# First half of the mixer's output projection: three bf16 terms and six products in place of two float32r terms and three

## The chip, the cores and the metric

One core of a Trainium2 chip runs the whole program. Its engines work side by side, each from a queue of its own: TensorE (in the profile PE for the products and PEld for loading the stationary operand), VectorE (DVE), ScalarE (ACT), GpSimd (POOL) and SyncE (SP), which here only starts transfers. The time is that of the device in microseconds (us) from the start to the end of one execution; lower is better. A comparison of two kernels uses several executions of each on the same chip.

## The reference

One inference step of a decoder layer (one layer) for a prompt of 512 tokens and 8 samples of 8 tokens, so 576 tokens in all, with 1024 features. The part that matters here is the mixer's output projection:

```python
u = _rms(x) * g_pre_mix
proj = u @ w_in
...
y_ssd = _rms(y_ssd.reshape(bsz, length, SSM_GROUPS, SSM_INNER // SSM_GROUPS)).reshape(bsz, length, SSM_INNER) * g_ssm_out
...
h_ml = _rms(h_ml).reshape(bsz, length, ML_INNER) * g_mlstm_out * jax.nn.sigmoid(og)
mix = jnp.concatenate([y_ssd.astype(x.dtype), h_ml.astype(x.dtype)], axis=-1) @ w_out
x = x + _rms(mix) * g_post_mix
```

`w_out` has 2048 rows and 1024 columns. Its first 1024 rows meet the output of the state-space heads (`y_ssd`), the last 1024 that of the mLSTM heads (`h_ml`). Everything is in float32, and the outputs are compared with a float32 computation. After the mixer come a cross attention and a gated feed-forward network (SwiGLU), both with projections of the same kind.

## The kernel before, in words

All activations lie feature by feature: 128 features on the partitions, 8 tiles of them, and the 576 tokens along the free axis. A large product is done in float32r with each operand as two terms: `hi` is the operand copied to a float32r tile on ScalarE, `lo` is the operand minus `hi`, made on VectorE (`split`, line 191, for activations, `split_w`, line 173, for weights). `gemm` (line 195) then issues three products for each input tile of 128 features: weight hi by activation hi (line 201), weight hi by activation lo (line 202), weight lo by activation hi (line 203). Each of them loads its stationary weights anew. The tokens go in two parts, 256 and 320 wide (`HALVES`), because a bank of PSUM holds 512 columns; `gemm2` (line 206) runs `gemm` for a part and evacuates the bank.

`split_w` takes a buffer `raw` (two of them) for the loaded float32 weights, and a pair `whi`, `wlo` (three pairs) of 128x1024. The load is issued on the SP queue. With `cut=1024` the whole subtraction is VectorE's.

The first half of the output projection is the loop at line 1133. For each of 8 output tiles it loads the weights' first 1024 rows (`I["wout"][j, 0]`, 8 input tiles of 128x128), splits them, runs both token parts, one in a bank of the pool `pg` (`GP`) and one in a bank of `pa` (`MP`), three banks in each, and copies each bank to `f_mix` on ScalarE (line 1136, `evs`). Its operand is `mixs`, the state-space output after its norm: `gn_apply` (line 1014) multiplies `y` by gain and norm row (line 1017) and splits it into `mixs_h` and `mixs_l` (line 1018). `mixs_h` lies in a pool on the right side (`big0`, line 1007) that opens where the pool of the mLSTM samples closes (its last operation is line 1002), `mixs_l` in slot 2 of the big buffers.

In the same loop `presplit` splits weights of later stages and writes the low terms to DRAM; it goes by the evacuations (`evs`). From the fifth output tile on, transfers of the memory inputs (`memraw`, line 1143) are issued behind the weight loads. The second half (`out2`, line 1166) adds the mLSTM rows: it multiplies `mixm_h` and `mixm_l` by the other 1024 rows of the weights, adds the bank to `f_mix` (line 1161) and collects sums of squares for the norm behind it (`ssqo`, line 1162, and `ssqm` for the memory, line 1150). It stays as it is.

Around this loop the order of the instructions on each engine is made by a planner that simulates the program and takes what is ready, in the order of the source; products into different banks are thus interleaved. Further on, from the second half of the attention's output projection, the order on each engine is written out by hand.

Of the kernel before, what the change touches and what calls it, by code (L numbers as in the profile page):

```python
# [11 lines left out]
F32 = mybir.dt.float32  # L12
F32R = mybir.dt.float32r
BF16 = mybir.dt.bfloat16
AF = mybir.ActivationFunctionType
ALU = mybir.AluOpType
# [3 lines left out]
P = 128  # L20
T = 576
# [3 lines left out]
KT = 8  # L25
# [3 lines left out]
HALVES = [(0, 256), (256, 320)]  # L29
# [87 lines left out]
def build(nc, tc, ctx, I, O):  # L117
    V, A, G, S, TE = nc.vector, nc.scalar, nc.gpsimd, nc.sync, nc.tensor
    mm = TE.matmul

    cp = ctx.enter_context(tc.tile_pool(name="const", bufs=1))
    wp = ctx.enter_context(tc.tile_pool(name="weights", bufs=1))
# [8 lines left out]
    def SL(slot, name, dt=F32, shape=(P, KT, T)):  # L131

        return big.tile(list(shape), dt, name=name, tag="s%d" % slot, bufs=1)
# [37 lines left out]
    loads = []  # L171

    def split_w(src, n=1024, cut=CUT, acc=False, pool=None, to=None, raw=None):
        if raw is None:
            raw = wp.tile([P, 1024], F32, name="raw", tag="raw", bufs=2)
        loads.append(S.dma_start(raw[:, :n], src))
        if to:
            split(*to, raw[:, :n])
            return to
        hi, lo = [(pool or wp).tile([P, 1024], F32R, name=k, tag=k, bufs=NWX if pool else 3) for k in ("whi", "wlo")]  # L180
        A.copy(hi[:, :n], raw[:, :n])  # L181
        for e, a, b in ((V, 0, cut), (G, cut, n)):
            if b > a and e is G and acc:

                A.activation(lo[:, a:b], hi[:, a:b].bitcast(F32), AF.Copy, scale=-1.0)  # L185
                G.dma_start(lo[:, a:b], src[:, a:b], accum_op=ALU.add)  # L186
            elif b > a:
                e.tensor_tensor(lo[:, a:b], raw[:, a:b], hi[:, a:b].bitcast(F32), op=ALU.subtract)  # L188
        return hi, lo

    def split(hi, lo, src, eng=None):
        A.copy(hi, src)
        (eng or V).tensor_tensor(lo, src, hi.bitcast(F32), op=ALU.subtract)
# [12 lines left out]
    def gemm2(units, xh, xl, evac, name, halves=(0, 1), alloc=None, order=None, parts=HALVES):  # L206
        for i in halves:
            t0, n = parts[i]
            ps = (alloc or GP)(name)[:, :n]
            m = gemm(ps, units, xh, xl, t0, n, order=order)  # L210
            evac(t0, n, ps)
        return m

    def act(t):
        return lambda k, t0, n: t[:, k, t0:t0 + n]


    pows, ssq_mm, rops, rows = [], [], [], []
# [124 lines left out]
    stop = gemm(ps0[2][1], [(*w2, KT)], U, UL, 256, 320, 0, NSS)  # L343
# [12 lines left out]
    stop = gemm(ps0[3][0], [(*w3, KT)], U, UL, 0, 256)  # L356
# [208 lines left out]
    y = xs  # L565
# [98 lines left out]
    for g in range(2):  # L664
        ps = BP("ps_xts")
# [5 lines left out]
    ps = BP("ps_bts")  # L671
# [7 lines left out]
    for g in range(2):  # L679
        for hb in range(2):  # L680
            dst = cpad[:, g, 4 * hb:4 * hb + 4, :].rearrange("p b t -> p (b t)")
            src = bc[:, 2 + g, TP + 32 * hb:TP + 32 * hb + 32]
# [4 lines left out]
    for g in range(2):  # L687
        psb = BP("ps_ls")
        pb3 = psb.rearrange("p (h t) -> p h t", h=8)
        for h in range(8):  # L690
            mm(psb[:, h * TS:(h + 1) * TS], sel[:80, 8 * g + h:8 * g + h + 1].to_broadcast([80, P]), cumst[:, TP:T],
               start=h == 0, stop=h == 7, skip_group_check=True)
# [8 lines left out]
        for h in range(8):  # L701
            k, j = h % 2, (8 * g + h) // 2
# [6 lines left out]
    ps = BP("ps_eg")  # L709
# [6 lines left out]
    for b in range(4):  # L716
# [3 lines left out]
        for g in range(2):  # L720
            for hb in (1, 0):
# [3 lines left out]
                   start=b == 0, stop=b == 3, skip_group_check=True)  # L725
        for hb in range(2):
# [4 lines left out]
            for g in range(2):  # L731
                ps = BP("ps_hu")
# [6 lines left out]
    ps = BP("ps_yt")  # L739
# [88 lines left out]
    for h in range(4):  # L828
        q, k = qk[:, h, :], qk[:, 4 + h, :]
# [16 lines left out]
        for c in range(4):  # L846
# [3 lines left out]
                        op=ALU.mult)  # L850
# [16 lines left out]
        f = head_norm(num, expnm[:, :, h:h + 1].rearrange("p c o -> p (c o)"), 4, mp_, "p")  # L867
# [89 lines left out]
    for hb in range(2):  # L957
# [6 lines left out]
        for b in range(4):  # L964
# [16 lines left out]
            for h in range(4):  # L981
                ps = BP("ps_cu")
# [13 lines left out]
        f = head_norm(num, ex, 1, ms, "s")  # L996
# [9 lines left out]

    big0 = ctx.enter_context(tc.tile_pool(name="big0", bufs=1, side="right", reuse_waits="tile"))

    def SL0(name, dt=F32R):
        return big0.tile([P, KT, T], dt, name=name, tag="s0", bufs=1)  # L1010

    mixs_h = SL0("mixs_h")
    mixs_l = SL(2, "mixs_l", F32R)
    def gn_apply(g):
        rb = gn_rc[g][0][:, 0:T]
        for j in range(4 * g, 4 * g + 4):
            V.scalar_tensor_tensor(y[:, j, :], y[:, j, :], PAR("g_ssm", j), rb, op0=ALU.mult, op1=ALU.mult)
            split(mixs_h[:, j, :], mixs_l[:, j, :], y[:, j, :])


    mixm_h = SL(3, "mixm_h", F32R)
# [77 lines left out]
    f = SL(5, "f_mix")  # L1099
# [8 lines left out]
    evs, ahead = [], []  # L1108
# [22 lines left out]
    rmem_b = at.tile([P, 256], F32, name="rmem_b")  # L1131
    ssqm, ssq = ssq_tile("ssqm"), ssq_tile("ssqo")
    for j in range(8):
        w = split_w(I["wout"][j, 0], cut=1024)
        for i, bank in enumerate((GP, MP)):
            gemm2([(*w, KT)], act(mixs_h), act(mixs_l), lambda t0, n, ps: evs.append(A.copy(f[:, j, t0:t0 + n], ps)),
                  "ps_o1", (i,), bank)
        presplit(1 if j else 2)

        if j > 3:  # L1140
            k2 = slice(2 * j - 8, 2 * j - 6)
            with tc.issue_after(loads[-1].ins):
                S.dma_start(memraw[:, k2, :], I["memT"][:, k2, :])
# [26 lines left out]
    x = SL(1, "x1")  # L1170
# [39 lines left out]
    m = out2(7, 0)  # L1210
    with tc.issue_after(m.ins):
        rc = rstd_cols([ssq], HCHUNKS[1], "po1", alloc=B0)
    m = out2(6, 0)
# [170 lines left out]
    mk, m = mem_key(3, wm[:2])  # L1384
    with tc.issue_after(m.ins):
        rc = rstd_cols([ssq], HCHUNKS[0], "po0", alloc=B0)
    mv, m = mem_value(3, wm[2:])
# [10 lines left out]
    m = xq(4, 1)  # L1398
    with tc.issue_after(m.ins):
        rc2[1] = rstd_cols([ssq2], HCHUNKS[1], "p21", alloc=B1)  # L1400
    m = xq(5, 1)
    with tc.issue_after(m.ins):
        rstd_rows(rc2[1][:, 2:3], CHUNKS[4:], rb2, B1)
    m = xq(6, 1)
# [34 lines left out]
    f = SL(4, "f_xo")  # L1439
# [250 lines left out]
    class Pair:  # L1690
# [72 lines left out]
        def bank(s):  # L1763
            return (MP if s.up else GP)("ps_u" if s.up else "ps_g")[:, :288]
# [726 lines left out]
```

## Time and profile before

| what | value |
|---|---|
| median of 3 runs | 1104.03 us (1101.62 to 1104.86) |
| the profiled execution: its own time | 1104.28 us |
| its span, first to last instruction | 1102.5 us |
| products (MATMUL) and loads (LDWEIGHTS) | 8351 each |
| busy: PE, PEld | 1089.3 us, 1042.0 us |
| busy: DVE, ACT, POOL | 771.4, 604.0, 215.3 us |
| first half of the projection (396.82 to 447.87 us) | 51.05 us, 384 products |
| second half (447.70 to 502.40 us) | 54.70 us |

In a row of the profile stand the line of the source, the engine, the operation, the tiles as output<-input, the shape as output<-input, and xN for the number of instructions. A row of the timeline begins with the start and the duration in us, counted from the span's start. A group's row ends with the busy time, the mean duration in ns, and the idle time in front of it with what ended it. A row of one tile has the least, median and greatest duration in ns and the first and last start in us. The duration of a product is the time until its result is there; products overlap, so the cost of one is the distance to the next start.

### The profile page before, as it was taken

The page shows a single profiled execution, that of the slowest core. Times are in us where ns is not written, and L with a number is a line of the kernel's source. Part 1 is how long each engine was busy: PE and PEld are TensorE (multiplying, and loading weights), DVE is VectorE, ACT ScalarE, POOL GpSimd, SP SyncE. Part 2 cuts the span into 40 slices and gives each one's busy share as a digit, 9 for nine tenths or more (in the row PEclk, how much of TensorE's full clock was granted, in tenths as well). Part 3 has the DMA queues.
Part 4 walks back from the last instruction along what each step waited for, and adds up shares of the span by engine and source line. Part 5 has one row for each costly group of instructions (what it writes and reads, how often), then busy time and mean ns, then how long its engine had stood idle before and what let it go on. Part 6 is the DMA issues. An engine that isn't in the chain of part 4 may idle for free.

```text
span 1102.5 us, 21225 instructions
## 1 busy us (share of the span) xinstructions
PE 1089.3 (99%) x8351; PEld 1042.0 (95%) x8351; DVE 771.4 (70%) x1521; ACT 604.0 (55%) x1121; POOL 215.3 (20%) x301
## 2 busy tenths in 40 slices
PE   9999999999999999999999999999999999999997
PEld 8999889898998999999988889999999999999997
DVE  6797765558786784578755556676578879888655
ACT  6768523246563465566535445634565556555654
POOL 1333442323122121110144401100000210020000
PEclk9999999999999999999999999999999999999999
DMA  6776553425474438773477755652552863497432
GB/s 205 178 148 154 121 160 126 155 83 158 130 202 108 127 99 287 284 278 100 154 272 268 287 168 169 208 184 66 179 152 82 203 161 89 102 230 211 108 133 86
DMA packets 59432, 182.34 MB, mean 165 GB/s; under 512 B 6556, under 2 KB 10780, under 8 KB 58820
## 3 DMA queue, kind: packets, MB, share of 16 engines
q1 hardware_dynamic: 44324, 142.19, 38.4%
q0 software_dynamic: 14720, 38.28, 16.6%
q8 instruction: 65, 1.06, 0.4%
q10 hardware_dynamic: 288, 0.52, 0.1%
q14 instruction: 35, 0.29, 0.1%
HBM read 151.66 MB, written 29.30 MB: 164 GB/s over the span
## 4 chain that ended last, share of the span: by engine, by line
PE 82%; DVE 5%; DMA 4%; ACT 3%; issue 1%; POOL 0%; DVEq 0%; ACTq 0%; SPq 0%
PE ps_in L201 5%; PE ps_in L202 5%; PE ps_in L203 5%; PE ps_g L1770 3%; PE ps_g L1771 3%; PE ps_g L1772 3%; PE ps_u L1770 3%; PE ps_u L1771 3%; PE ps_u L1772 3%; PE ps_o L201 2%; PE ps_o L203 2%; PE ps_o L202 2%; PE ps_dn L201 2%; PE ps_dn L203 2%; PE ps_dn L202 2%; PE ps_dn L1978 2%
## 5 line engine op out<-in xcount | busy, mean ns | idle before, releaser
L203 PE MATMUL ps_in<-uh,wlo 128*128 128x256 f32 (+1 forms) x544 | 163.8, 301 | 0.7 <-DMA wlo<-win 0.4
L202 PE MATMUL ps_in<-ul,whi 128*128 128x256 f32 (+1 forms) x544 | 163.9, 301 | 0.0
L201 PE MATMUL ps_in<-uh,whi 128*128 128x256 f32 (+1 forms) x544 | 163.7, 301 | 0.0
L181 ACT CAST whi<-raw 128x1024 fp32r<-128x1024 f32 (+1 forms) x102 | 102.7, 1011 | 83.5 <-PE ps_in L202 28.7
L188 DVE TENSOR_TENSOR wlo<-raw,whi 128x512 fp32r<-128x512 f32 (+1 forms) x94 | 91.2, 972 | 50.6 <-ACT whi L181 48.8
L202 PEld LDWEIGHTS ps_in<-ul,whi 128*128 128x128 f32 x544 | 103.0, 189 | 2.9 <-issue 2.2
L203 PEld LDWEIGHTS ps_in<-uh,wlo 128*128 128x128 f32 x544 | 103.0, 190 | 2.4 <-DVE wlo L188 0.6
L201 PEld LDWEIGHTS ps_in<-uh,whi 128*128 128x128 f32 x544 | 103.0, 189 | 2.0 <-issue 0.8
L186 POOL DMA_DIRECT2D wlo<-win x32 | 28.0, 883 | 80.8 <-ACT wlo L185 64.2
L1770 PE MATMUL ps_g<-b,whi 128*128 128x288 f32 x144 | 42.5, 296 | 0.2 <-ACT cc L1829 0.2
L1771 PE MATMUL ps_u<-b,whi 128*128 128x288 f32 x144 | 42.5, 295 | 0.0
L1771 PE MATMUL ps_g<-b,whi 128*128 128x288 f32 x144 | 42.5, 295 | 0.0
L1770 PE MATMUL ps_u<-b,whi 128*128 128x288 f32 x144 | 42.5, 295 | 0.0
L201 PE MATMUL ps_xo<-qh,whi 128*128 128x288 f32 x128 | 38.3, 302 | 0.4 <-ACT whi L181 0.3
L203 PE MATMUL ps_o<-mixm_h,wlo 128*128 128x256 f32 (+1 forms) x128 | 38.1, 298 | 0.0
L201 PE MATMUL ps_o<-mixm_h,whi 128*128 128x256 f32 (+1 forms) x128 | 38.0, 297 | 0.0
L202 PE MATMUL ps_o<-mixm_l,whi 128*128 128x256 f32 (+1 forms) x128 | 37.9, 296 | 0.0
L203 PE MATMUL ps_xq<-u2h,wlo 128*128 128x320 f32 (+1 forms) x128 | 37.9, 296 | 0.0
L202 PE MATMUL ps_xq<-u2l,whi 128*128 128x320 f32 (+1 forms) x128 | 37.8, 297 | 0.0
L201 PE MATMUL ps_xq<-u2h,whi 128*128 128x320 f32 (+1 forms) x128 | 37.8, 300 | 0.0
L202 PE MATMUL ps_xo<-ql,whi 128*128 128x288 f32 x128 | 37.7, 295 | 0.0
L203 PE MATMUL ps_xo<-qh,wlo 128*128 128x288 f32 x128 | 37.5, 295 | 0.0
(785 smaller groups left out, 3895.3 us busy)
## 6 DMA issues: line engine op xcount, KB each, us to landing
raw<-win SPq DMA_DIRECT2D x35, 512.0 KB, 3.6
raw<-wout SPq DMA_DIRECT2D x17, 512.0 KB, 5.6
raw<-wxq SPq DMA_DIRECT2D x13, 512.0 KB, 3.7
raw<-wgate SPq DMA_DIRECT2D x13, 512.0 KB, 4.4
raw<-wup SPq DMA_DIRECT2D x13, 512.0 KB, 4.0
wlo<-win POOLq DMA_DIRECT2D x24, 256.0 KB, 5.6
kva<-kc SPq DMA_DIRECT2D x12, 512.0 KB, 6.5
kva<-vc SPq DMA_DIRECT2D x12, 512.0 KB, 6.6
```

What stands on the lines that cost most here:

```text
L181: A.copy(hi[:, :n], raw[:, :n])
L186: G.dma_start(lo[:, a:b], src[:, a:b], accum_op=ALU.add)
L188: e.tensor_tensor(lo[:, a:b], raw[:, a:b], hi[:, a:b].bitcast(F32), op=ALU.subtract)
L201: mm(ps, wh, ah, start=i == 0, stop=False)
L202: mm(ps, wh, al, start=False, stop=False)
L203: m = mm(ps, wl, ah, start=False, stop=i == len(tiles) - 1)
L1770: mm(ps, wh, b[0][:, k, :], start=start and k == 0, stop=False, skip_group_check=True)
L1771: mm(ps, wh, b[1][:, k, :], start=False, stop=False, skip_group_check=True)
L1772: m = mm(ps, wl, b[0][:, k, :], start=False, stop=k == 3, skip_group_check=True)
L1978: mm(ps, wh, bh, start=start and k == 0, stop=False, skip_group_check=True)
```

## The change

The operand and the weights of the first half are split into three bf16 terms (high, middle, low) in place of two float32r terms. Six products take the place of three: high weights by high, middle and low operand, middle weights by high and middle, low weights by high. The residues are formed in place, in the buffer that held the operand: `y` for the activations, `raw` for the weights. The three terms of the weights share the two old buffers (a 128x2048 bf16 tile has the bytes of a 128x1024 float32r tile). The three terms of the operand lie in the two old places: high and middle together on the right side, low in slot 2. The copies from the banks, the loads, `presplit` and everything behind the loop keep their text.

```diff
+    def split3(dst, x):
+
+        h, m, l = dst
+        A.copy(h, x)
+        V.tensor_tensor(x, x, h, op=ALU.subtract)
+        A.copy(m, x)
+        V.tensor_tensor(l, x, m, op=ALU.subtract)
+
+    def split3_w(src):
+
+        raw = wp.tile([P, 1024], F32, name="raw", tag="raw", bufs=2)
+        loads.append(S.dma_start(raw, src))
+        a, b = [wp.tile([P, 2048], BF16, name=k, tag=k, bufs=3) for k in ("whi", "wlo")]
+        w = a[:, 0:1024], a[:, 1024:2048], b[:, 0:1024]
+        split3(w, raw)
+        return w
+
+    def gemm3(banks, w, x3, parts):
+
+        for k in range(KT):
+            for i, wt in enumerate(w):
+                for ps, (t0, n) in zip(banks, parts):
+                    for xt in x3[:3 - i]:
+                        mm(ps, wt[:, k * P:(k + 1) * P], xt[:, k, t0:t0 + n], start=k == 0 and i == 0 and xt is x3[0],
+                           stop=k == KT - 1 and i == 2)
...
-    def SL0(name, dt=F32R):
-        return big0.tile([P, KT, T], dt, name=name, tag="s0", bufs=1)
-
-    mixs_h = SL0("mixs_h")
-    mixs_l = SL(2, "mixs_l", F32R)
+    def SL0(name, dt=F32R, kt=KT):
+        return big0.tile([P, kt, T], dt, name=name, tag="s0", bufs=1)
+
+    mixs = SL0("mixs_hm", BF16, 2 * KT)
+    mixs = mixs[:, 0:KT, :], mixs[:, KT:2 * KT, :], SL(2, "mixs_l", BF16, (P, 2 * KT, T))[:, 0:KT, :]
     def gn_apply(g):
         rb = gn_rc[g][0][:, 0:T]
         for j in range(4 * g, 4 * g + 4):
             V.scalar_tensor_tensor(y[:, j, :], y[:, j, :], PAR("g_ssm", j), rb, op0=ALU.mult, op1=ALU.mult)
-            split(mixs_h[:, j, :], mixs_l[:, j, :], y[:, j, :])
+            split3([t_[:, j, :] for t_ in mixs], y[:, j, :])
...
     for j in range(8):
-        w = split_w(I["wout"][j, 0], cut=1024)
-        for i, bank in enumerate((GP, MP)):
-            gemm2([(*w, KT)], act(mixs_h), act(mixs_l), lambda t0, n, ps: evs.append(A.copy(f[:, j, t0:t0 + n], ps)),
-                  "ps_o1", (i,), bank)
+        w = split3_w(I["wout"][j, 0])
+        banks = [bank("ps_o1")[:, :n] for bank, (_, n) in zip((GP, MP), HALVES)]
+        for ps, p in zip(banks, HALVES):
+            gemm3([ps], w, mixs, [p])
+            evs.append(A.copy(f[:, j, p[0]:p[0] + p[1]], ps))
         presplit(1 if j else 2)
```

## The prediction

> **What bounds the kernel now.** I read the busy shares of the page first, then the stages around the change (busy time of each engine between the first product of one accumulation and the first of the next), then the instructions of the changed tile group by shape, then single starts on TensorE, and last the list of waits.
>
> ```profile
> core 0: 1102.5 us, clock 0.999
> PE 1089.3 (99%) x8351; PEld 1042.0 (95%) x8351; DVE 771.4 (70%) x1521; ACT 604.0 (55%) x1121; POOL 215.3 (20%) x301
> ...
> 396.70:447.70 51.00, 51.00 (x385) 50.94 (x385) 33.23 (x44) 32.42 (x56) 8.98 (x15) 1.00 0.66 233
> 447.70:502.40 54.70, 53.48 (x402) 52.91 (x401) 36.19 (x63) 34.28 (x58) 8.16 (x15) 1.00 0.74 260
> ```
>
> TensorE is busy 1089.3 of 1102.5 us, at a granted clock of 0.999. In the two stage rows the columns after the window are its length and then the busy time of PE, PEld, DVE, ACT and POOL. The first row is the half that is changed: TensorE never rests, while VectorE and ScalarE work 33 and 32 of 51 us. The second row, the other half of the projection, is left as it is. So the question is what TensorE has to stream, and the first fact to get is the rate of a product.
>
> ```profile
> 396.82 0.69 PE L201 MATMUL ps_o<-mixs_h,whi 128*128 128x256 f32 x4
> 397.35 0.37 PE L202 MATMUL ps_o<-mixs_l,whi 128*128 128x256 f32 x1
> 397.57 0.28 PE L203 MATMUL ps_o<-mixs_h,wlo 128*128 128x256 f32 x1
> 397.68 0.28 PE L201 MATMUL ps_o<-mixs_h,whi 128*128 128x256 f32 x1
> 397.80 0.31 PE L202 MATMUL ps_o<-mixs_l,whi 128*128 128x320 f32 x1
> 397.95 0.31 PE L203 MATMUL ps_o<-mixs_h,wlo 128*128 128x320 f32 x1
> 398.10 0.31 PE L201 MATMUL ps_o<-mixs_h,whi 128*128 128x320 f32 x1
> 398.24 0.28 PE L202 MATMUL ps_o<-mixs_l,whi 128*128 128x256 f32 x1
> ...
> 447.87 0.31 PE L201 MATMUL ps_o<-mixm_h,whi 128*128 128x320 f32 x1
> ```
>
> The second column (0.28, 0.31) is how long one product is in flight; the cost is the distance of the starts. A 256-column product is followed after 0.11 to 0.12 us, a 320-column one after 0.14 to 0.15. The half begins at 396.82 and ends at 447.87: 51.05 us for 8 output tiles x 8 input tiles x 2 parts x 3 products = 384 products, 132.9 ns each on a mean of 288 columns. A float32r product thus already streams 2.17 columns in a nanosecond. The trace labels these products f32; they are not slow ones.
>
> **The change part by part.** *Products.* The 384 float32r products go, 768 bf16 ones come (six for three), half of them 256 columns wide, half 320. The kernel has few bf16 products, but two groups run back to back: the end of the warm-up, where the granted clock is 1.00 (first row, the column after PEld), and the small decay rows:
>
> ```profile
> 4.86:5.42 0.56, 0.56 (x8) 0.49 (x5) 1.00 1.06 220
> ...
> L300 PE MATMUL ps_warm<-wz x8: 272/273/421, 4.4 to 5.4; 128*128 128x256 bf16 x8
> L300 PEld LDWEIGHTS <-wz x5: 98/98/98, 4.9 to 5.3; 128*128 128x128 bf16 x5
> ...
> 5.08 0.49 PE L300 MATMUL ps_warm<-wz 128*128 128x256 bf16 x3
> ...
> 113.83 0.41 PE L691 MATMUL ps_ls<-cumst,c 80*128 80x64 bf16 x8
> 114.08 0.36 PE L203 MATMUL ps_in<-uh,wlo 128*128 128x256 f32 x1
> ```
>
> Three 256-column products last 0.49 us from the first start to the last end. One is in flight 0.273, so the starts are (0.49 - 0.273) / 2 = 0.109 us apart. Eight 64-column products, each with another stationary, start from 113.83 on and the next instruction at 114.08: 31 ns each. From 64 to 256 columns the price rises by 78 ns, 0.406 ns a column. For 320 columns the line through both gives 135 ns, in proportion to 256 it is 136; I take 136. The half is then 384 x 0.109 + 384 x 0.136 = 41.9 + 52.2 = 94.1 us, and with 51.05 taken away **+43.0 us**. Bounds: if a product cost only the slope (104 and 130 ns) it would be 89.9 us, +38.8; if bf16 kept the 132.9 ns of the float32r products, for instance because loading a different full stationary costs the array the same, 102.1 us, +51.0. The 64-column row with eight different stationaries is nearest to what is issued, so I stay at 0.109 and 0.136. None of this lies beside other work: the row of this stage has TensorE busy in all 51.00 us.
>
> The Trainium skill, page "TensorE: Matmul & The Clock Gate", section "Back-to-back issue gap", gives a warm gap of N/2.4 + 2.5 ns, and the warm-up row agrees with it (109 ns at 256). The same section states that in real streams of loads and products the spacing was 81 ns at N=128 and 131 ns at N=512; by that, an estimate of about 102 ns at 288 columns, the sum would be +27 us instead of +43. What that rule would be in this kernel stands under the rivals.
>
> *Splitting the weights.* Per output tile one cast and one subtraction become two and two, with the same 1024 elements:
>
> ```profile
> L188 DVE TENSOR_TENSOR wlo<-raw,whi 128x1024 fp32r<-128x1024 f32 x8 | 9.8, 1219 | 0.9 <-ACT whi L181 0.9
> ...
> L181 ACT CAST whi<-raw x2: 1047/1049/1051, 382.2 to 389.4; 128x1024 fp32r<-128x1024 f32 x2
> L188 DVE TENSOR_TENSOR wlo<-raw,whi x2: 1216/1220/1224, 383.7 to 390.5; 128x1024 fp32r<-128x1024 f32 x2
> ...
> 384.93 25.59 SPq L176 DMA_DIRECT2D raw<-wout  x4
> ```
>
> That adds 8 x 1.05 = 8.4 us on ScalarE and 8 x 1.22 = 9.8 us on VectorE. A cast to bf16 and a subtraction with a bf16 operand of this size are in no row; between half these prices and twice them, they stay 4 to 20 us. I take the same price, for the element count is the same. They lie under 94 us of products: VectorE comes to 33 + 10 + 6 (below) = 49 of 94 us, ScalarE to 32 + 8 + 5 = 45. Without that cover they would cost 18 us. The four steps of one tile run one after the other, 1.05 + 1.22 + 1.05 + 1.22 = 4.5 us, against 11.8 us of products per output tile, with three weight buffers. The raw buffer is let go one cast and one subtraction (2.3 us) later, since the first residue is written into it. Behind a weight load that waits for it stand the later loads on the SP queue, of which the memory inputs and the next weights are the nearest; with two raw buffers and 11.8 us per tile, nobody waits for those 2.3 us. Loads and bytes are unchanged.
>
> *Splitting the operand.* Eight tiles of 576 columns get a second cast and a second subtraction:
>
> ```profile
> 395.55 0.37 ACT L1002 COPY qk<-ps_hts 128x256 f32<-128x256 f32 x1 [0.28 <-PE ps_hts L1001]
> 395.82 4.69 ACT L192 CAST mixs_h<-xs 128x576 fp32r<-128x576 f32 x8
> ...
> L192 ACT CAST mixs_h<-xs x8: 668/670/678, 395.8 to 399.8; 128x576 fp32r<-128x576 f32 x8
> L193 DVE TENSOR_TENSOR mixs_l<-xs,mixs_h x8: 747/750/759, 396.5 to 401.6; 128x576 fp32r<-128x576 f32 x8
> ...
> L1136 ACT COPY f_mix<-ps_o x16: 352/394/422, 406.0 to 455.3; 128x256 f32<-128x256 f32 x8, 128x320 f32<-128x320 f32 x8
> ```
>
> This is the one place with little cover. All eight splits start only at 395.8, right after line 1002, when the buffer on the right side comes free, and the first product follows at 396.82. In the old kernel the low term of tile 0 is there at 396.5 + 0.75 = 397.3, just when four products with the high term are through and the fifth starts (397.35). In the new one the middle term is ready at 395.82 + 0.67 + 0.75 + 0.67 = 397.9 at the earliest, the low one at 398.7. TensorE has four open banks (two output tiles, two parts), so four products with the high term, 0.49 us, end at 397.3; it rests about 0.6 us to 397.9, does four more, and rests about 0.3 to 398.7. From tile 1 on, four banks keep it 24 x 0.1225 = 2.9 us per input tile, and even with no overlap a tile's four steps take 2.84. So **+1.0 us**; bounds 0 (other products get there first) and, if only one output tile's weights were split in time, see the rivals. The first evacuation writes the buffer that the splits read; it was at 406.0 and comes later (four banks x 8 tiles end near 420), the last residue near 395.8 + 8 x 2.84 = 418.5, so that hazard costs nothing.
>
> *Given back.* The longer half leaves room for the work that runs late in the next one:
>
> ```profile
> PE ps_ss L226 <- DVE ssqm L267: 1.2, 1, 1.2
> ```
>
> This 1.2 us wait near 481 us is the only idle time of TensorE in the unchanged half, behind VectorE's sums for the memory inputs. With 43 us more for VectorE it can vanish; between 0 and -1.2 I take **-0.6**. All TensorE idle of the kernel is 1102.5 - 1089.3 = 13.2 us, so even all of it could not pay for the products.
>
> Sum on the profiled execution: 1104.28 + 43.0 + 1.0 - 0.6 = **1147.7 us** (its span is 1102.5, 1.8 us lie around it and stay). That execution is 0.25 us over the median 1104.03 of the runs, which I leave out as smaller than the rest.
>
> **The rivals.**
> *bf16 keeps the fixed part of float32r.* A float32r product costs 132.9 ns for 288 columns, 0.406 x 288 = 117 of it streaming. If the other 16 belong to any change of a full stationary, the half is 102.1 us: 1104.28 + 51.0 + 1.0 = 1156.3. For it: the warm-up reloads one and the same stationary. Against it: the 64-column row, 31 ns with a load each.
>
> *The front starves.* If the second output tile's weights are not split by 396.8 (before: cast at 389.4, subtraction at 390.5, now 2.3 us and some queueing more), TensorE has only 1.47 us of work per input tile against up to 2.84 of splitting: 8 x 1.37 = 11 us more, 1158.7. Against it: 391.7 + 2.3 = 394.0 leaves 2.8 us.
>
> *The loads set the spacing.* If overlapped products in a long stream start as fast as their stationaries load, 98 ns by the load row above, the half is 768 x 0.098 = 75.3 us: 1104.28 + 24.2 + 0.4 = 1128.9. Against it: eight 64-column products follow each other at 31 ns with such loads, so the load is no clock, and at 256 columns the warm-up keeps 109. The section of the Trainium skill named above would be near this case; no row here bears it out.
>
> *Not slower: two products in the array at once.* The samples' attention shows products that do overlap:
>
> ```profile
> 594.36 0.64 PE L1345 MATMUL ps_sa<-kva,qsm 128*32 128x256 f32 x8
> 594.82 0.61 PE L1345 MATMUL ps_sa<-kvb,qsm 128*32 128x256 f32 x8
> ```
>
> Eight 256-column products in 0.46 us are 58 ns each; they use 32 columns of the array each. If three bf16 products in a row on one stationary could overlap in pairs, 61 ns each, the half would take 47.0 us: 1104.28 - 4.0 + 0.4 = 1100.7. It decides from 51.05 / 768 = 66.5 ns on. Against it: the warm-up is just such a row on one full stationary, and it does not.
>
> *The change does not do what it says* would mean fewer than 768 products or loads in the half.
>
> ```profile
> L201 PEld LDWEIGHTS ps_o<-mixs_h,whi x128: 187/187/193, 396.7 to 447.3; 128*128 128x128 f32 x128
> ...
> L202 PEld LDWEIGHTS ps_o<-mixs_l,whi x128: 186/187/194, 397.3 to 447.4; 128*128 128x128 f32 x128
> ```
>
> Against it: the first two float32r products of a step share a stationary, and each still has a load of its own, 128 and 128. A chance is not set aside for it.
>
> **How the numbers follow.** Forecast 0.78, the fixed part 0.07, the starved front 0.06, the loads 0.03, the overlap 0.02; 0.04 are for an order of instructions elsewhere that changes by more than a few us, since most of the program is ordered by a planner. The range goes from the slope alone (1104.28 + 38.8 + 0.4 = 1143.5) to the fixed part (1156.3, rounded up): 1143.5 to 1156.5. A measurement of this kernel tells 0.3% (3.3 us) from nothing. Faster 0.02 is the overlap, no change 0.01, slower 0.97 the rest.
>
> **What would show it.** In the changed profile: 768 bf16 products in the half, starts 0.109 and 0.136 us apart, the half some 94 to 95 us; loads of about 98 ns in place of 187; a rest of about 1 us on TensorE right after the first four products; VectorE near 49 and ScalarE near 45 us in it; the unchanged half 53.5 to 54.7 us. The prediction is wrong if the spacing in the half isn't within 117 to 133 ns on the mean, if TensorE rests over 5 us in it, or if another stage moves by more than 3 us.

## The result and the profile after

| | before | after |
|---|---|---|
| median | 1102.82 us (4 runs, 1101.59 to 1104.86) | 1164.64 us (4 runs, 1162.08 to 1165.85) |
| ratio, 95% interval | | 1.0545 [1.0519, 1.0572] |
| the profiled execution: its own time | 1104.28 us | 1163.91 us |
| its span | 1102.5 us | 1162.1 us |
| the changed half of the projection | 51.05 us | 110.6 us |

The changed kernel is slower by 5.5%, 61.8 us. The forecast was 1147.7 us and its range ended at 1156.5: the direction was right, the time was not. The page of the changed kernel begins with the span, the busy engines and, in 40 slices of 29 us, the clock that was granted to TensorE:

```profile
span 1162.1 us, 22029 instructions
...
PE 1137.7 (98%) x8735; PEld 1069.6 (92%) x8735; DVE 786.8 (68%) x1537; ACT 617.7 (53%) x1137; POOL 215.7 (19%) x301
...
PEclk9999999999999889999999999999999999999999
```

There are 384 products and 384 loads more, as the change says. New is the dent in the last row: in the slices from 378 to 436 us, where the changed half begins, the clock is not full. The list of TensorE's waits of the changed kernel (engine, line that waited, what it waited for: us in total, times, longest) says why:

```profile
PE ps_o L240 <- ACT mixs_hm L222: 6.4, 1, 6.4
PE ps_o L240 <- ACT mixs_hm L220: 4.3, 1, 4.3
PE ps_o L240 <- DVE mixs_l L223: 2.3, 1, 2.3
PE ps_ss L1533 <- DVE ssqxo L1609: 1.5, 1, 1.5
```

The first three, 13.0 us, are one wait each for the high (L220), the middle (L222) and the low term (L223) of the operand. The kernel before had nothing of the kind. The stage view divides the half by it (window, length, then busy time of PE, PEld, DVE, ACT and POOL, granted clock):

```profile
396.27:412.75 16.48, 3.41 (x15) 1.72 (x13) 16.35 (x28) 16.48 (x30) 4.13 (x6) 0.58 0.21 73
412.75:416.20 3.45, 3.45 (x16) 2.25 (x16) 3.45 (x6) 1.20 (x3) 0.00 (x0) 0.51 0.71 280
416.20:506.95 90.75, 90.75 (x744) 72.46 (x741) 29.29 (x32) 28.53 (x44) 7.49 (x14) 1.00 0.42 143
506.95:560.10 53.15, 53.15 (x401) 52.90 (x400) 35.70 (x63) 33.77 (x57) 5.51 (x10) 1.00 0.61 209
```

The first window begins at 396.27, where the next product could have started (the two products ahead of it start at 396.11 and keep TensorE busy to 396.49). In it, TensorE is busy 3.4 of 16.5 us, while VectorE and ScalarE are busy without a break. In the second it is busy throughout, at half the clock. In the third it streams at the full clock without a rest: 28 of the 768 products have started by 416.2, and the other 740 start between 416.29 and 506.89, where the next half begins: 90.6 us, 122.4 ns each. The fourth is the unchanged half.

The half therefore is 110.6 us (396.27 to 506.89) = 94.1 us of products, as priced, and 16.5 us at its front. Of these, 13.0 are the three waits. Most of the remaining 3.5 is the clock: 28 products at twice the distance are at most 28 x 0.1225 = 3.4 us. The whole difference of the spans, 59.6 us, is: products +43.05, front +16.5, start of the half -0.55 (396.27 in place of 396.82), unchanged half -1.4, all behind it +2.0. The last is the fourth wait above, 1.5 in place of 0.5 us, and a second drop of the clock behind it (764.29 to 767.71 us, 3.4 us at half speed, 1.7 lost), less some 0.7 us gained on the way.

What the front waited for is seen in the order in which ScalarE and VectorE did the splitting. ScalarE first, in the timeline of the changed kernel (start, duration):

```profile
396.43 1.06 ACT L220 CAST whi<-raw 128x1024 bf16<-128x1024 f32 x1
397.37 2.56 ACT L1057 ACTIVATE mixm_h<-qk,ghalf 128x512 fp32r<-128x512 f32 x4
399.83 0.36 ACT L1028 COPY qk<-ps_hts 128x256 f32<-128x256 f32 x1
400.09 4.69 ACT L220 CAST mixs_hm<-xs 128x576 bf16<-128x576 f32 x8
404.67 0.79 ACT L961 ACTIVATE tmp<-tmp 128x256 f32<-128x256 f32 x2
405.35 1.95 ACT L1057 ACTIVATE mixm_h<-qk,ghalf 128x512 fp32r<-128x512 f32 x3
407.19 1.04 ACT L222 CAST whi<-raw 128x1024 bf16<-128x1024 f32 x1
408.12 4.70 ACT L222 CAST mixs_hm<-xs 128x576 bf16<-128x576 f32 x8
```

VectorE, in the same timeline:

```profile
401.64 5.43 DVE L221 TENSOR_TENSOR xs<-xs,mixs_hm 128x576 f32<-128x576 f32 x8
406.99 0.75 DVE L963 SCALAR_TENSOR_TENSOR qk<-tmp,qk 128x256 f32<-128x256 f32 x2
407.88 0.42 DVE L1062 SCALAR_TENSOR_TENSOR ogs<-ogs,qk 128x256 f32<-128x256 f32 x1
408.22 2.07 DVE L1058 SCALAR_TENSOR_TENSOR mixm_l<-qk,ghalf,mixm_h 128x512 fp32r<-128x512 f32 x3
410.21 0.68 DVE L1063 TENSOR_TENSOR ogs<-ogs,ghalf 128x512 f32<-128x512 f32 x1
410.81 1.22 DVE L223 TENSOR_TENSOR wlo<-raw,whi 128x1024 bf16<-128x1024 f32 x1
411.94 5.43 DVE L223 TENSOR_TENSOR mixs_l<-xs,mixs_hm 128x576 bf16<-128x576 f32 x8
```

Two things stand there. The operand is split in waves: the high terms of all eight tiles (400.09), then all residues (401.64), then all middle terms (408.12), then all low terms (411.94); a product that needs the middle term of tile 0 waits for a wave that comes after the high terms of tile 7. And work for later stages lies between: the copy L1028 that frees the place of `mixs_hm` (before: L1002, at 395.55) stands behind a weight cast and four casts of `mixm_h` and starts at 399.83; three more casts of `mixm_h` and a weight cast stand ahead of the middle wave. TensorE shows the same from its side:

```profile
396.11 0.38 PE L1027 MATMUL ps_hts<-c,hns 128*128 128x128 f32 x2
400.82 1.60 PE L240 MATMUL ps_o<-mixs_hm,whi 128*128 128x256 bf16 x6 [4.33 <-ACT mixs_hm L220]
408.85 1.60 PE L240 MATMUL ps_o<-mixs_hm,whi 128*128 128x256 bf16 x6 [6.44 <-ACT mixs_hm L222]
412.75 0.37 PE L240 MATMUL ps_o<-mixs_l,whi 128*128 128x256 bf16 x1 [2.30 <-DVE mixs_l L223]
```

Six banks are open, where the forecast counted four. Each takes one product with the high term, and then all six wait for the middle wave.

### The profile page after: what moved, and what is told of

Same layout as the page of the kernel before. It is cut to its first block, busy times and chain, and to the rows that moved or that the text cites. A ratio compares the mean times of both kernels' runs of the same rounds, so it can differ in the third digit from the quotient of the medians.

```text
span 1162.1 us, 22029 instructions
## 1 busy us (share of the span) xinstructions
PE 1137.7 (98%) x8735; PEld 1069.6 (92%) x8735; DVE 786.8 (68%) x1537; ACT 617.7 (53%) x1137; POOL 215.7 (19%) x301
## 4 chain that ended last, share of the span: by engine, by line
PE 84%; DVE 4%; ACT 3%; DMA 2%; issue 1%; POOL 1%; DVEq 0%; ACTq 0%; POOLq 0%
PE ps_o L240 8%; PE ps_in L201 5%; PE ps_in L202 5%; PE ps_in L203 5%; PE ps_g L1797 3%; PE ps_g L1798 3%; PE ps_g L1799 3%; PE ps_u L1797 3%; PE ps_u L1798 3%; PE ps_u L1799 3%; PE ps_dn L201 2%; PE ps_v L808 2%; PE ps_v L806 2%; PE ps_v L807 2%; PE ps_dn L203 2%; PE ps_dn L202 2%
## 5 line engine op out<-in xcount | busy, mean ns | idle before, releaser
L181 ACT CAST whi<-raw 128x1024 fp32r<-128x1024 f32 (+1 forms) x94 | 94.4, 1008 | 99.8 <-PE ps_in L202 24.9
L188 DVE TENSOR_TENSOR wlo<-raw,whi 128x512 fp32r<-128x512 f32 (+1 forms) x86 | 81.5, 949 | 75.4 <-ACT whi L181 73.6
L240 PE MATMUL ps_o<-mixs_hm,whi 128*128 128x320 bf16 (+1 forms) x512 | 96.8, 292 | 10.8 <-ACT mixs_hm L222 6.4
L240 PEld LDWEIGHTS <-whi 128*128 128x128 bf16 x640 | 63.7, 100 | 30.9 <-issue 13.9
L240 PE MATMUL ps_o<-mixs_l,whi 128*128 128x256 bf16 (+1 forms) x128 | 37.0, 289 | 2.3 <-DVE mixs_l L223 2.3
```

The lines of the kernel that those rows point to most:

```text
L240: mm(ps, wt[:, k * P:(k + 1) * P], xt[:, k, t0:t0 + n], start=k == 0 and i == 0 and xt is x3[0], stop=k == KT - 1 and i == 2)
```

## The experiments

Three questions were open. Is the front, and its order, what the forecast lacked, or do the products cost more in the stream than the profile showed? Is the rate of the products priced rightly against float32r? And is there a form of the idea that is not slower? Where one time is given for a kernel, it is of one run, beside a median of the kernel before on the same chip of 1102.38 us (1103.27 us for the doubled products); the others have intervals.

**The splits in turn.** In the changed kernel, the high cast of tile j+2 is queued behind the last two steps of tile j.

```diff
+    terms = []
...
-            split3([t_[:, j, :] for t_ in mixs], y[:, j, :])
+            terms.append(split3([t_[:, j, :] for t_ in mixs], y[:, j, :], terms[-2] if len(terms) > 1 else ()))
```

In `split3`, the first cast and residue are issued after (`tc.issue_after`) what is handed in.

> The changed kernel, with one thing else: the four steps that split an operand tile (high cast, first residue, middle cast, low residue) are queued tile by tile, the cast of tile j+2 behind the middle cast of tile j, in place of all high casts, then all middle casts. Theory A (the 16.5 us that the half takes beyond its 94.1 us of products are made by the order of the splits at its front and by what stands ahead of them): the first product stays near 400.8 us, but the middle term of tile 0 no longer waits for eight high casts; the three mixm casts, two gate evacuations and a weight cast that the planner puts between still do. The gap of 6.9 us before the second wave shrinks to some 4.5, the one before the low term to under 1.5; the half 110.6 -> about 105, the time about 1158. Rival B (the splits are simply twice the work for VectorE and ScalarE, and no order helps): within 3 us of the changed kernel, 1161 to 1167.

Measured: 1158.53 us, 6.1 less than the changed kernel. The list of waits of this kernel:

```profile
PE ps_o L242 <- ACT mixs_hm L223: 4.3, 1, 4.3
PE ps_o L242 <- ACT mixs_hm L225: 3.0, 1, 3.0
...
PE ps_o L242 <- DVE mixs_l L225: 0.9, 1, 0.9
```

The wait for the first high term (here L223) is untouched; those for the middle and the low term (L225) are 3.9 in place of 8.7 us. The time is what was expected, but partly by luck. The half was to fall to about 105 us and falls to 107.0 (396.55 to 503.54), so the waves cost 3.6 us: the waits are 4.8 shorter, but more products run at half the clock. Some 2 us more are gained behind the projection, where the wait of 1.5 us for `ssqxo` is 0.4 and the clock does not fall.

**Later work behind the splits.** In the changed kernel, the casts and residues of `mixm` are queued behind the last split of the operand; the waves stay.

```diff
+    behind = ExitStack()
+    for ins in terms[-1]:
+        behind.enter_context(tc.issue_after(ins.ins))
     for j in range(8):
         hm = qk[:, 4 * (j % 2) + j // 2, 0:TP]
...
     split(mixm_h[:, :, TP:T], mixm_l[:, :, TP:T], ogs)
+    behind.close()
```

> The changed kernel, with one thing else: the casts and residues of the other half's operand (mixm) are queued behind the last split of this half's operand; the splits keep their order of waves. Theory A: four mixm casts (2.6 us) go from ahead of the copy that frees the right-side buffer, so the first product comes at about 398.4 in place of 400.8, and three more go from between the waves; the gap before the middle term shrinks from 6.9 to about 5.5 us and still pulls the clock down. The half 110.6 -> about 104, the time about 1157. Rival B: 1161 to 1167.

Measured: 1155.84 us, 8.8 less. The half takes 104.6 us (397.47 to 502.08), 6.0 less, and begins 1.2 us later; some 3 us of the 8.8 are gained behind the projection, where the `ssqxo` wait is gone. The first product starts at 399.59 in place of 400.82, and in the list of waits of this kernel both other waits are shorter too:

```profile
PE ps_o L239 <- ACT mixs_hm L222: 5.3, 1, 5.3
PE ps_o L239 <- ACT mixs_hm L220: 1.9, 1, 1.9
...
PE ps_o L239 <- DVE mixs_l L222: 0.5, 1, 0.5
```

**Both.** The two edits together.

```diff
+            terms.append(split3([t_[:, j, :] for t_ in mixs], y[:, j, :], terms[-2] if len(terms) > 1 else ()))
...
+    for ins in terms[-1]:
+        behind.enter_context(tc.issue_after(ins.ins))
```

> The changed kernel with both: splits tile by tile, and mixm behind them. Theory A: first product near 398.4, gaps of 2.1 and about 2.5 us, none over 3.4, so the granted clock stays at 1.00 in the half; the half 99 us, the time about 1152 (11 to 12 us under the changed kernel, some 48 over the kernel before). If the product price of the prediction is right as well, what is left over the kernel before is 43 us of products and about 5 of waiting. Rival B: 1161 to 1167. Rival C (the clock falls because bf16 products come dense, not because TensorE rests): the clock still falls to half in the half.

Measured: 1151.34 us (1150.86 to 1152.02), ratio 1.0446 [1.0429, 1.0464]. The times add to less (6.1 + 8.8 = 14.9, together 13.3), since the 2 to 3 us behind the projection are in each of them. In the half itself the gains do not overlap: it takes 99.5 us (397.13 to 496.63), 11.1 less, for 3.6 + 6.0. Two waits of 1.9 us are left, 3.7 us in place of 13.0. The expectation that the clock would no longer fall was wrong: it was at half for one stretch of 3.41 us behind 401.41, although no gap was that long. Two windows show it, the one ahead of the fall and the one at half clock:

```profile
398.00:401.41 3.41, 0.90 (x6) 0.58 (x6) 3.41 (x7) 3.41 (x8) 0.91 (x4) 1.00 0.00 0
401.41:404.82 3.41, 2.82 (x13) 1.77 (x13) 3.41 (x6) 2.91 (x6) 1.43 (x3) 0.50 0.65 210
```

**The front cleared.** To both edits, two orders are added: the second output tile's weight splits go behind VectorE's last step for the mLSTM samples, the third's behind the first operand tile.

```diff
-        w = split3_w(I["wout"][j, 0])
+        with ExitStack() as later:
+            for ins in ((), (hns,), terms[0])[j] if j < 3 else ():
+                later.enter_context(tc.issue_after(ins.ins))
+            w = split3_w(I["wout"][j, 0])
```

> The kernel with tile-by-tile splits and mixm behind them, with the weight splits moved out of the way too: the second output tile's residues behind the last VectorE operation of the mLSTM samples (line 1024 of the changed kernel), the third tile's split behind the first operand tile's. Theory A: what still holds the first product back there (399.25 against 396.82 before) is one weight residue of 1.2 us on VectorE and one weight cast of 1.05 us on ScalarE, ahead of the copy that frees the buffer; without them the first product comes at about 397 and the time falls by another 2 to 3 us, to 1148 to 1149.5, which is the 43 us of products and about 2 of waiting. Rival: the start is held by something else (a transfer, the samples' own chain); then the time stays at 1151 within 1 us.

Measured: 1147.06 us (1146.56 to 1148.14), ratio 1.0387 [1.036, 1.0414]. TensorE's timeline in this kernel, and then the stage:

```profile
396.82 0.31 PE L203 MATMUL ps_in<-uh,wlo 128*128 128x320 f32 x1
396.97 0.66 PE L242 MATMUL ps_o<-mixs_hm,whi 128*128 128x256 bf16 x4
398.39 0.65 PE L242 MATMUL ps_o<-mixs_hm,whi 128*128 128x256 bf16 x4 [0.76 <-ACT mixs_hm L225]
399.76 0.27 PE L242 MATMUL ps_o<-mixs_l,whi 128*128 128x256 bf16 x1 [0.72 <-DVE mixs_l L225]
```

```profile
396.97:492.75 95.78, 94.31 (x771) 75.08 (x769) 47.93 (x61) 45.10 (x72) 10.59 (x20) 1.00 0.47 162
```

The half now begins right behind the work before it, with four open products, a rest for the middle and a rest for the low term, and the clock stays at 1.00. It takes 95.78 us, 94.1 of products and 1.7 at the front. The bf16 products stream there as in the changed kernel, so it is not the bf16 products that pull the clock down. The time is 0.6 us under the forecast, but that is close partly by luck: the front was 1.7 us for 1.0, the unchanged half gave back 1.4 for 0.6, and 1.0 was gained behind the projection. With the same products and the same splits, in another order, the changed kernel is 17.6 us faster. Its front costs 1.7 us in place of 16.5, so 14.8 of those 16.5 us are an order, not a price of the arithmetic; most of the rest of the gain lies behind the projection (599.0 us in place of 602.0).

**Three of the six products.** In the changed kernel, the products with a low term are left out (the terms are still made), so the output lacks them.

```diff
-                    for xt in x3[:3 - i]:
+                    for xt in x3[:2 - i]:
...
-                           stop=k == KT - 1 and i == 2)
+                           stop=k == KT - 1 and i == 1)
```

> The changed kernel with three of the six products (high by high, high by middle, middle by high); the low terms are still made, but their three products are left out, so the output lacks them. By the product price of 0.109 and 0.136 us the half has 47.0 us of products in place of 94.1. The front waits only for the middle term (to about 408.8, not 412.7), so the half takes some 59 us and the time comes to about 1112. If the price of a bf16 product depended on the row of six (three products on one stationary), the spacing in the trace would move by over 5 ns from 109 and 136.

Measured: 1113.86 us. The waits for the high and the middle wave are those of the changed kernel, 4.3 and 6.4 us, and the half takes 56.7 us from its first product (400.79 to 457.48). Counted from 396.24, where it could have begun, it takes 61.2, where some 59 were expected. With as many products as the kernel before and nearly the front of the changed one, the kernel is still 11.5 us slower than before: 14.2 us of front remain beside 47.0 us of products, so most of the front's price does not depend on the six products. Nor does the price of a product depend on the row of six: from 420 us on, some 306 products take 37.5 us, 122 to 123 ns each.

**Twice the float32r products.** In the kernel before, each product of the half is issued twice, so that its output is doubled.

```diff
...
-            mm(ps, wh, ah, start=i == 0, stop=False)
-            mm(ps, wh, al, start=False, stop=False)
-            m = mm(ps, wl, ah, start=False, stop=i == len(tiles) - 1)
+            for r in range(twice + 1):
+                mm(ps, wh, ah, start=i == 0 and not r, stop=False)
+                mm(ps, wh, al, start=False, stop=False)
+                m = mm(ps, wl, ah, start=False, stop=i == len(tiles) - 1 and r == twice)
...
```

> The kernel before, with each float32r product of the first half issued twice into the same bank (768 in place of 384; the half's output is doubled). This is six float32r products, with no third term and no further split. By 132.9 ns a product the half takes 102.1 us, 51 more, and the time is about 1153.5. By the spacings of the trace a bf16 product is 10 ns cheaper, so the changed kernel's 94.1 us of products should be some 8 us below this half. If the spacing of float32r products fell when the same stationary comes back at once, the half would be nearer to 94.

Measured: 1154.54 us. Two rows of the stage view of this kernel, the half and the one behind it:

```profile
397.82:499.81 101.99, 101.99 (x770) 101.93 (x769) 35.26 (x45) 33.91 (x57) 11.65 (x20) 1.00 0.43 148
499.81:553.00 53.19, 53.19 (x402) 52.94 (x401) 35.74 (x63) 33.59 (x57) 5.50 (x10) 1.00 0.61 209
```

768 float32r products take 102.0 us, without a rest and at the full clock; 768 bf16 products took 94.1. A bf16 product saves 10 ns of 133, and six for three cost 43 us. This kernel, with more work for TensorE, is faster than the changed one; its front is the old one, without a wait. Its second half took 53.2 us as well.

**Two bf16 terms.** In the kernel before, both operands become two bf16 terms with three products.

```diff
-    mixs_h = SL0("mixs_h")
-    mixs_l = SL(2, "mixs_l", F32R)
+    mixs_h = SL0("mixs_h", BF16, 2 * KT)[:, 0:KT, :]
+    mixs_l = SL(2, "mixs_l", BF16, (P, 2 * KT, T))[:, 0:KT, :]
...
-        w = split_w(I["wout"][j, 0], cut=1024)
+        w = split_bw(I["wout"][j, 0])
```

> The kernel before, with both operands of the first half as two bf16 terms (high, low) and three products: same number of products and of splits, another type. It keeps 16 bits of each operand, where two float32r terms keep more. Product price theory: 384 products take 47.0 us in place of 51.05, so the time falls by 4.0 us, 0.36%, to about 1098.5. Rival (the front is sensitive to bf16 as such): a gap of some us at 396 to 403, no gain.

Measured: 1105.85 us (1103.44 to 1107.61), ratio 1.0012 [0.9994, 1.003]: no gain, against the expectation. The stage rows and the first wait of this kernel:

```profile
396.84:443.80 46.96, 46.96 (x387) 37.50 (x385) 31.52 (x43) 30.45 (x54) 8.46 (x14) 1.00 0.61 213
443.80:505.20 61.40, 55.66 (x401) 54.79 (x400) 37.71 (x65) 35.70 (x60) 8.66 (x16) 0.94 0.75 262
```

```profile
PE ps_ss L237 <- DVE ssqm L278: 5.7, 1, 5.7
```

The half is 4.1 us shorter, as the price of a product says. The other half is 6.9 us longer: the wait for the memory inputs' sums, 1.2 us before, is 5.7 (477.1 to 482.8), and the clock is at half from 480.1 to 486.9.

**Two bf16 terms, the memory norm later.** To that kernel, the norm that waits for those sums is moved behind the last output tiles.

```diff
-    memory_norm()
     for j in range(4, 8):
         out2(j, 1)
+    memory_norm()
```

> Two bf16 terms and three products as before in this study, and the memory norm's sums on TensorE (two one-column products per bank, 1.2 us of waiting in the kernel before, 5.7 with two bf16 terms) are queued behind the four next products' groups of the second half in place of ahead of them. Theory: the 4.1 us that the first half gains came back as a longer wait for VectorE's sums over the memory, which go by the transfers of weights in the second half and not by TensorE; 27 us later in the queue these sums are ready. Then the gain stands: 4.1 and the old 1.2 us, some 1097 us (0.995 of before). Rival: the half is bounded by its transfers in another place too, and the time stays at 1101 to 1103.

Measured: 1103.17 us (1101.22 to 1106.56), ratio 0.9998 [0.9981, 1.0016]. Its waits and its second half:

```profile
PE ps_o L201 <- ACT whi L181: 2.4, 1, 2.4
...
PE ps_o L203 <- DVE wlo L188: 0.7, 1, 0.7
```

```profile
443.53:501.85 58.32, 55.22 (x401) 54.46 (x400) 37.68 (x66) 35.58 (x60) 8.79 (x16) 0.97 0.78 275
```

The wait for the sums is gone, and TensorE waits for the weights' terms instead. The second half ends nearly where it ended before (502.5 us there, 501.85 here), and 1.4 us later than with that move alone (500.48, in the next run): the whole 4.1 us are lost there. That what feeds this half sets its end nearly as early as TensorE does is the reading of these waits; no run shows it by itself.

**That move alone**, in the kernel before.

```diff
-    memory_norm()
     for j in range(4, 8):
         out2(j, 1)
+    memory_norm()
```

> The kernel before with that move alone. Theory: the wait of 1.2 us goes, 1101 us (0.999 of before, at the edge of what can be told). Rival: unchanged, or slower where the later place meets a late VectorE queue.

Measured: 1102.11 us (1100.06 to 1108.35), ratio 0.9988 [0.997, 1.0007]: no change that the times can tell. In the profiled execution the 1.2 us wait is gone and the second half takes 53.1 us (447.34 to 500.48).

**Mixed terms.** The product of the high terms stays float32r, the two cross products become bf16, with bf16 copies of the high terms made on ScalarE; the work on `mixm` is queued behind the operand's splits.

```diff
...
+            mm(ps, wh, ah, start=k == 0, stop=False)
+            mm(ps, wb, al, start=False, stop=False)
+            mm(ps, wl, ab, start=False, stop=k == KT - 1)
...
```

> The kernel before, with the high product in float32r and the two cross products in bf16 (high weights as bf16 by the low operand as bf16, low weights as bf16 by the high operand as bf16); the extra bf16 copies are casts on ScalarE that wait for no residue, and mixm is queued behind the operand's split. Only one load in three is a float32r one. If the 10 ns that a float32r product costs more stand at the product in front of a float32r load, the half falls by 256 x 0.0104 = 2.7 us, to 48.4, and the time to about 1099.7 (0.24%). If they stand at the float32r product itself, it is the same sum; if each change of type costs more than 10 ns, the time rises.

Measured: 1106.33 us (1104.88 to 1111.99), ratio 1.0029 [1.0011, 1.0047], slower by 0.3% where a gain was expected. Two things are in it. The half begins late, at 399.46, behind a wait of 2.7 us for the first high term, and the clock is at half from 399.4 to 402.8. And the products are no cheaper. The timeline of TensorE in this kernel, with the float32r product on L238:

```profile
415.15 0.36 PE L238 MATMUL ps_o<-mixs_h,whi 128*128 128x256 f32 x1
415.36 0.28 PE L239 MATMUL ps_o<-mixs_lb,wlo 128*128 128x256 bf16 x1
415.48 0.27 PE L240 MATMUL ps_o<-mixs_lb,wlo 128*128 128x256 bf16 x1
415.51 0.36 PE L238 MATMUL ps_o<-mixs_h,whi 128*128 128x256 f32 x1
...
416.57 0.36 PE L238 MATMUL ps_o<-mixs_h,whi 128*128 128x256 f32 x1
```

Four triples in 1.42 us are 0.355 us each. Three float32r products of this width take 3 x 0.118 = 0.354 (in the kernel with doubled products, 18 starts between 414.83 and 416.95). Two bf16 products in a triple thus save nothing here: the bf16 product behind a float32r one starts 0.21 us after it, and the float32r one 0.03 us after the bf16 one before it.

**Mixed terms with the front and the memory norm ordered.** The same, with the bf16 casts in turn, the weights' splits later as in the cleared front, and the norm moved.

```diff
...
+        with tc.issue_after(after.ins) if after else ExitStack():
+            a = A.copy(h, x)
+        with tc.issue_after(a.ins):
+            c = A.copy(b, x)
...
-    memory_norm()
     for j in range(4, 8):
         out2(j, 1)
+    memory_norm()
```

> Float32r for the high product and bf16 for the two cross products, with the move of the memory norm, the bf16 copies of the operand cast in turn with the high terms, the second output tile's residue behind the samples' last VectorE operation and the third tile's split behind the second operand tile's. Theory: without the late start (399.5 in place of 396.8) and the clock step, 2.7 us of products and 1.2 us of waiting are gained: some 1098.5 us (0.9965 of before). Rival: at changes between float32r and bf16 stationaries TensorE loses more than the 10 ns; then it stays at 1101 or more.

Measured: 1104.86 us (1103.64 to 1109.14), ratio 1.0011 [0.9992, 1.003]. The half begins at 396.36 again and the clock stays full, but it takes 52.4 us, 1.7 of them waits for the weights' terms, and the other 55.8: no gain was there to be kept. No form of the change that was tried is faster than the kernel before.

## Why the prediction was right in its main term and wrong in its time

- **What bounds the half.** Right. TensorE streams 90.75 of 90.75 us once the operand is there, and VectorE and ScalarE lie under it: 49.1 and 46.2 us over the whole half (the first three stage rows added), forecast 49 and 45. In the 16.5 us at the front it is the other way round: there these two are never idle and TensorE waits.
- **Products, +43.0.** Right: 122.4 ns on the mean, forecast 122.5. The cleared front shows it whole, 94.1 us of a half of 95.78. Three rivals fall with it: the doubled float32r products stay at 132.8 ns (102.0 us / 768), so bf16 does not keep their fixed part, and the products follow neither the 98 ns of the loads nor an overlap in pairs.
- **Splitting the weights, 0.** As forecast in time: no wait of TensorE in the half names the weights' terms. But the step priced it by the work of the whole half and not by the place of each instruction. A weight cast of 1.06 us stands ahead of the copy at 399.83, another of 1.04 ahead of the middle wave, a residue of 1.22 ahead of the low one. Putting two tiles' splits later brought 4.3 us (from both edits to the cleared front).
- **Splitting the operand, +1.0, bounds 0 and the starved front.** This is the step that failed. It took three things from the old trace: that the first split starts at 395.8, "right after line 1002"; that a tile's four steps follow each other ("the middle term is ready at 395.82 + 0.67 + 0.75 + 0.67 = 397.9 at the earliest"); and so two rests of 0.6 and 0.3 us. In the changed kernel the first split starts at 400.09, the middle cast of tile 0 at 408.12 and its low residue at 411.94. Measured in place of 1.0 are 16.5 us: 13.0 of waits and some 3.4 of the clock, which the step didn't price. The sum of the durations was right. The four open banks that it counted were six, and "at the earliest" was used as a forecast, though the order on these two engines comes from a planner. Where the order was made nearly what the step assumed, the front cost 1.7 us and the time was 1147.06. That the planner took the waves because all high casts were ready while the middle ones still waited is argued, not shown.
- **Given back, -0.6.** Measured -1.4 (53.15 for 54.53 us); the wait is gone, and 0.2 more. Doubled products (53.19) and the moved norm (53.14) give the same second half, so it is what remains there without that wait.
- **The starved front, 1158.7.** Its place was right and its size the nearest of the rivals (11 us, measured 16.5), but that is luck. Its cause was wrong: it needed the second output tile's weights to be late, and they were not what TensorE waited for. It had been set against an order of the operand's splits that was never put in doubt.
- **Not priced: another stage.** +2.0 us behind the projection, of which a wait of 1.5 us and the clock behind it are most. Over the kept profiles, this part takes 598.5 to 602.0 us, 600.0 before and 602.0 in the changed kernel; that wait was 0.4 us or less in the kernels with a better front and with three products, and no run isolates its cause.

The sum with the measured front: 1104.28 + 43.05 + 16.5 - 0.55 - 1.4 + 2.0 = 1163.9, the time of the profiled execution. Of the marks that the prediction set for itself, the spacing held, no other stage moved by more than 3 us, and "if TensorE rests over 5 us in it" came true. The range was too narrow at its upper end: the 0.04 that were left to the planner were for an order elsewhere, and none for its order at this front.

## What to carry to other kernels

A step that becomes longer, ahead of an engine that was never idle, is to be priced at the place where its first result is needed: ask in which order the other engines will take its parts and what else stands in their queues there, not only how much they have to do in the stage. Where a planner makes that order, price the worst one too (here all high terms, then all middle ones), add the clock that TensorE loses at the gap, and write the order out if the difference matters. Replacing three products by six needs products at less than half the price, and the distance of the starts in the trace says beforehand that bf16 is no such product beside float32r at these widths.

## What the runs showed of the hardware

**The clock falls at gaps shorter than its window.** The stretches at half clock were 17.07 us (changed kernel, front), 13.65 (splits in turn), 10.24 (later work behind), 3.41 (both) and none with the two rests of 0.8 and 0.7 us in the cleared front: whole multiples of 3.41 us. The Trainium skill, page "TensorE: Matmul & The Clock Gate", section "What's actually happening", gives such a window (3413 ns, running freely) and has the clock at half after at least one idle window. The length agrees. The condition does not quite. In the 3.41 us ahead of the fall, TensorE was busy 0.83 us in the changed kernel's front (395.65 to 399.06), 0.90 with both edits (398.00 to 401.41: a rest, six products, and 1.3 us of the next rest), and 1.89 around the 1.5 us wait in the timeline below (760.88 to 764.29). So a window need not be wholly idle. Where the limit lies, no run here shows.

```profile
761.01 0.29 PE L203 MATMUL ps_u<-u3h,w 128*128 128x288 f32 x1
762.81 0.83 PE L1533 MATMUL ps_ss<-c,ssqxo 128*128 128x1 f32 x6 [1.52 <-DVE ssqxo L1609]
...
764.44 0.44 PE L201 MATMUL ps_g<-u3h,w 128*128 128x288 f32 x1
764.68 0.44 PE L202 MATMUL ps_g<-u3l,w 128*128 128x288 f32 x1
```

From 764.4 on, the products start 0.24 us apart, where 0.13 is usual.

**Mixing types keeps the price of float32r.** A triple of one float32r and two bf16 products took 0.355 us against 0.354 for three float32r ones, although a bf16 product in a row of its kind takes 0.109. Why the change of type costs what the type saves was not tested.

**A stage with two limits close together.** Taking 4.1 us from TensorE's products ended in no gain (1105.85 us, and 1103.17 with the norm later); adding 43 us gave 1.4 back. That the gain is lost in the next stage was shown by one move (the wait went and another came). That its loads and splits hold its end there is argued, not followed to its last cause.
